# Layer 0's shift and scale computed transposed on TensorE, by column blocks, with the first projections accumulating over these blocks

## The chip, the cores and the metric

The kernel runs on one core of a Trainium2 chip. The metric is the device time of one execution in microseconds, the median of several runs. The kernel before takes 2007.55 us (three runs, 2006.95 to 2007.87).

## What is computed

The reference is one inference step of two trunk layers over 9 tiles of 128 tokens (tile 0 the context tokens, conditioned by `c_ctx`; tiles 1 to 8 the latent tokens, conditioned by `c`). D_MODEL is 1024. What this case touches is the head of each layer:

```python
mod = (silu(cvec) @ w_mod + b_mod)                 # w_mod: 1024 x 3072
shift, scale, gate = split(mod, 3)
h = rms_norm(x, g_pre) * (1.0 + scale) + shift
fx, fz, rq, rk, rv, rz, aq, ak, av, az, mg = split_columns(h @ w_in)
```

Three branches follow (Fourier mixing, retention, windowed attention), each gated, then a merge, an output projection and the residual.

## The kernel before

Activations are kept transposed, as `HH` and `HL` (model dimension on 128 partitions by 8 row blocks k, tokens along the free dimension): a rounded part and the remainder, so that a product with split weights `hi`, `lo` takes three matmuls (`proj_n`, L228 HH by hi, L229 HH by lo, L230 HL by hi). A weight unit is loaded into a `raw` buffer (two of them), split by ACT (L174, the rounded part) and POOL (L175, the remainder). Units of group 1 (columns `C_RK` to +512, two row blocks of 512 columns each) are loaded at L203 (`unit_n2`) in runs of 2 KB; units of the next sections at L188 (`unit_t`: 128 columns of all 1024 rows, runs of 512 bytes).

Layer 0 begins with `startup` (L285 on). SP issues all loads here, in the order of the program as its scheduler arranged it.

1. Three x tiles (L287) are loaded and normalised (`prep`: L254 sum of squares on ACT, L246 on DVE and L248 on POOL for the reciprocal root, L256 multiply on DVE), transposed on PE (L308), copied to `xT` by ACT (L309).
2. `w_mod` comes in 16 row blocks of 128 x 1024 (L325, `stage`, rows of 4 KB): eight of the scale, then eight of the shift. For the scale, DVE accumulates block by block for both conditionings (L335, L337), PE transposes (L345), DVE reduces (L346) and forms `sm` = (1 + scale) g_pre (L347, L348) and multiplies xT (L353). For the shift, PE multiplies `siluc` by the block (L360, output of 2 rows by 512 columns); the result is copied (L366), transposed (L369), and `sh` formed (L370). Then HH (ACT, L377) and HL (DVE, L378) of tiles 0 to 2.
3. Group 1 (`nat_group`, L519 on): for each of nine tiles, 24 matmuls of `proj_n` into one bank, then an evacuation with rotary embedding on DVE (`rope`, L491, L497, L501) and a store. Its first step loads the four weight units, in the midst of the shift's blocks (`GK`). Tiles 3 to 5 and 6 to 8 are loaded, prepared, and finished (`finish`: L387 on DVE, L388 HH on ACT, L390 HL on DVE or POOL) in chunks of three while earlier tiles are projected.

Behind group 1 come the DFT matmuls of the Fourier ring (L637) and then a long run of other projections (L218 to L220) and branches, in both layers, which the change leaves as it is.

Of the kernel before, what the change touches and what calls it, by code (L numbers as in the profile page):

```python
# [16 lines left out]
P = 128  # L17
D = 1024
# [13 lines left out]
GK = 3  # L32
# [50 lines left out]
def hybrid_step(ctx, tc, ins, cst, outs):  # L83
# [20 lines left out]
    def mk(pl, shape, tag, dt=F32, **kw):  # L104
        return pl.tile(shape, dt, tag=tag, name=nm(tag), **kw)
# [177 lines left out]
    def startup(first):  # L283
        with pool("st", side="right") as st:
            def load_x(t):  # L285
                xt = mk(st, [P, D], "x0", bufs=3)
                SP.dma_start(xt, ins["x_prompt"][0] if t == 0 else ins["x_sample"][0, (t - 1) * P : t * P, :])  # L287
                return xt

            xts = [load_x(t) for t in range(3)]  # L290
# [27 lines left out]
            wms = {}

            def stage(n):  # L320
                k, c0 = n % KT, 0 if n >= KT else D
                if n % 3 == 0:
                    wms["big"] = chunk("big", 2).rearrange("p a b -> p (a b)")
                wm = wms["big"][:, n % 3 * D : n % 3 * D + D]
                last_w[0] = SP.dma_start(wm, w_mod[0, k * P : (k + 1) * P, c0 : c0 + D]).ins  # L325
                return wm

            for k in range(KT):
                wm = stage(k)
                if k == 2:  # L330
                    SP.dma_start(bm, b_mod[0, 0 : 2 * D].rearrange("(s k p) -> p s k", p=P, k=KT))
                    SP.dma_start(gpr, g_pre[0].rearrange("(k p) -> p k", p=P))
                for s in range(2):
                    if k == 0:
                        DVE.tensor_scalar(dacc[s], wm, siluc[:, k, s : s + 1], None, op0=ALU.mult)  # L335
                    else:
                        DVE.scalar_tensor_tensor(  # L337
                            out=dacc[s], in0=wm, scalar=siluc[:, k, s : s + 1], in1=dacc[s], op0=ALU.mult, op1=ALU.add
                        )
            pr = mk(st, [P, KT, 2], "dred")  # L340
            for c in range(0, KT, 2):
                pt = (sc if c % 4 else sl)([P, 2, 2, P])
                for cc in range(2):
                    for s in range(2):
                        PE.transpose(pt[:, cc, s, :], dacc[s][:, (c + cc) * P : (c + cc + 1) * P], ident)  # L345
                DVE.tensor_reduce(pr[:, c : c + 2, :], pt, axis=AX.X, op=ALU.add)  # L346
            DVE.tensor_tensor(out=sm, in0=pr, in1=bm[:, 1, :].unsqueeze(2).to_broadcast([P, KT, 2]), op=ALU.add)  # L347
            DVE.scalar_tensor_tensor(  # L348
                out=sm, in0=sm, scalar=1.0, in1=gpr.unsqueeze(2).to_broadcast([P, KT, 2]), op0=ALU.add, op1=ALU.mult
            )  # L350
            for k in range(KT):
                for s, tok in ((0, slice(0, P)), (1, slice(P, CH))):
                    DVE.tensor_scalar(xT[:, k, tok], xT[:, k, tok], sm[:, k, s : s + 1], None, op0=ALU.mult)  # L353
            for k in range(KT):
                wm = stage(KT + k)
                if k == GK:
                    with tc.issue_after(last_w[0]):
                        next(first)
                for i in range(2):
                    PE.matmul(  # L360
                        macc[i], siluc[:, k, :], wm[:, i * 512 : i * 512 + 512], start=(k == 0), stop=(k == KT - 1)
                    )
            last = last_w[0]
            mr = mk(st, [P, D], "xh", bufs=2)
            for i in range(2):
                (DVE.tensor_copy if i else ACT.copy)(mr[:2, i * 512 : i * 512 + 512], macc[i])  # L366
                pt = tr([P, 4, 2])
                for c in range(4):
                    PE.transpose(pt[:, c, :], mr[:2, (4 * i + c) * P : (4 * i + c + 1) * P], ident[:2, :2])  # L369
                DVE.tensor_tensor(  # L370
                    out=sh[:, 4 * i : 4 * i + 4, :], in0=pt,
                    in1=bm[:, 0, 4 * i : 4 * i + 4].unsqueeze(2).to_broadcast([P, 4, 2]), op=ALU.add,
                )
            for s, tok in ((0, slice(0, P)), (1, slice(P, CH))):
                for k in range(KT):
                    b = sh[:, k, s : s + 1]
                    ACT.activation(HH[:, k, tok], xT[:, k, tok], AF.Identity, bias=b)  # L377
                    DVE.scalar_tensor_tensor(  # L378
                        out=HL[:, k, tok], in0=xT[:, k, tok], scalar=b, in1=f(HH[:, k, tok]),
                        op0=ALU.add, op1=ALU.subtract,  # L380
                    )
# [10 lines left out]
            xT = chunk("big", 2)  # L392
            for t in range(3, 6):
                with tc.issue_after(last):
                    xt = load_x(t)
                prep(t, xt, xT)
            next(first)
            finish(3, 6, 1, xT)
            xT = chunk("big", 2)
            for t in range(6, NT):  # L400
                with tc.issue_after(last):
                    xt = load_x(t)
                prep(t, xt, xT)
                next(first)
            finish(6, NT, 1, xT)
# [98 lines left out]
    for l in range(DEPTH):  # L504
# [56 lines left out]
        if l == 0:  # L561
            startup(g1)
# [730 lines left out]
```

## Time and profile before

| what | value |
|---|---|
| median of three runs | 2007.55 us |
| the profiled execution's own time | 2009.5 us |
| its span in the trace | 2007.7 us |
| mean granted TensorE clock | 0.989 of full speed |
| PE busy | 1955.6 us, 97% of the span |
| DVE, ACT, POOL busy | 51%, 34%, 27% of the span |
| chain that ended last | PE 87%, DMA 5%, DVE 4% |
| first projection of group 1 begins | 48.08 us |
| first matmul behind group 1 begins | 106.98 us |

The profiled execution lies 1.95 us above the median, and 1.8 us of it are outside the span. Times below are microseconds from the start of the span. A PE record of the form L228 lasts 0.39 us though the next begins 0.23 us later: matmuls are pipelined, and for work back to back the distance of the starts counts. The granted clock is given as a share of full speed: 1.00 is 2.4 GHz, 0.50 is 1.2 GHz.

### The profile page before, as it was taken

The numbers are of one execution on the slowest core, as the hardware profiler recorded it, in microseconds if no ns is written. First come the engines' busy times: TensorE is split into PE (matmuls) and PEld (weight loads), VectorE is DVE, ScalarE is ACT, GpSimd is POOL, SyncE is SP. The second block draws the span as 40 slices with busy tenths as digits, with TensorE's granted clock in tenths as the row PEclk, the third lists the DMA queues.
The fourth block names the chain that finished last, engine by engine and source line by source line (L and its number), as shares of the span: only waits on it lengthen the run. The fifth ranks groups of instructions, "written<-read, shape, count | busy, mean of one in ns | idle before, by whom it ended". The sixth has DMA issues, their size and how long they took to land.

```text
span 2007.7 us, 30798 instructions
## 1 busy us (share of the span) xinstructions
PE 1955.6 (97%) x11334; PEld 1815.4 (90%) x11334; DVE 1027.7 (51%) x2675; ACT 678.0 (34%) x1563; POOL 550.0 (27%) x424
## 2 busy tenths in 40 slices
PE   5999899999999999999999999999999999999998
PEld 2898788999999999999878978899999999999987
DVE  6726557556677774204675362444556655520411
ACT  3522111234454544214331211022445554421411
POOL 2222232112122222534441204122211222233342
PEclk8999999999999999999999999999999999999999
DMA  8323554353344333324344235234332433242142
GB/s 293 103 72 99 132 159 135 110 166 114 103 120 128 109 105 108 108 86 134 118 132 102 59 94 162 74 115 131 119 95 78 122 95 104 87 144 83 57 154 86
DMA packets 245191, 230.59 MB, mean 115 GB/s; under 512 B 37920, under 2 KB 215856, under 8 KB 244784
## 3 DMA queue, kind: packets, MB, share of 16 engines
q1 hardware_dynamic: 245040, 228.62, 37.9%
q8 instruction: 89, 1.46, 0.3%
q14 instruction: 62, 0.51, 0.1%
HBM read 170.14 MB, written 58.42 MB: 114 GB/s over the span
## 4 chain that ended last, share of the span: by engine, by line
PE 87%; DMA 5%; DVE 4%; issue 1%; ACT 1%; SPq 1%; POOL 0%; DVEq 0%; POOLq 0%; ACTq 0%
PE pj L218 13%; PE pj L220 13%; PE pj L219 13%; PE pj L228 5%; PE pj L229 5%; PE pj L230 5%; PE pv L1118 4%; PE tr L1111 3%; PE sl L1057 2%; PE sl L960 2%; PE sl L962 2%; PE sl L961 2%; PE pj L960 2%; PE pj L962 2%; PE pj L961 2%; PE sl L230 2%
## 5 line engine op out<-in xcount | busy, mean ns | idle before, releaser
L218 PE MATMUL pj<-HH,uh 128*128 128x384 f32 x1440 | 493.4, 343 | 8.9 <-DVE XL L653 3.9
L220 PE MATMUL pj<-HH,ul 128*128 128x384 f32 x1440 | 488.8, 339 | 0.0
L219 PE MATMUL pj<-HL,uh 128*128 128x384 f32 x1440 | 487.3, 338 | 0.0
L175 POOL TENSOR_TENSOR ul<-raw,uh 128x1024 fp32r<-128x1024 f32 x80 | 192.9, 2412 | 489.3 <-ACT uh L174 375.6
L218 PEld LDWEIGHTS pj<-HH,uh 128*128 128x128 f32 x1440 | 272.3, 189 | 13.2 <-DVE XL L653 4.2
L219 PEld LDWEIGHTS pj<-HL,uh 128*128 128x128 f32 x1440 | 272.1, 189 | 0.5
L220 PEld LDWEIGHTS pj<-HH,ul 128*128 128x128 f32 x1440 | 272.2, 189 | 0.3
L446 DVE SCALAR_TENSOR_TENSOR macc<-mw,siluc,macc 128x256 f32<-128x256 f32 x224 | 139.3, 664 | 10.5 <-DMA mw<-in_w_mod 10.5
L174 ACT CAST uh<-raw 128x1024 fp32r<-128x1024 f32 x80 | 84.0, 1050 | 168.0 <-PE pj L219 112.5
L228 PE MATMUL pj<-uh,HH 128*128 128x512 f32 x336 | 135.1, 403 | 5.2 <-DVE xh L1253 2.6
L229 PE MATMUL pj<-ul,HH 128*128 128x512 f32 x336 | 133.9, 399 | 0.0
L230 PE MATMUL pj<-uh,HL 128*128 128x512 f32 x336 | 133.7, 398 | 0.0
L1094 ACT ACTIVATE E<-E,NM 128x640 f32<-128x640 f32 (+1 forms) x128 | 101.8, 798 | 56.9 <-DVE NM L1090 56.4
L963 DVE SCALAR_TENSOR_TENSOR M<-M,sl 128x384 f32<-128x384 f32 x48 | 26.6, 554 | 183.1 <-PE sl L962 182.6
L1114 ACT CAST Eh<-tr 128x512 fp32r<-128x512 f32 (+1 forms) x136 | 76.2, 575 | 101.8 <-PE tr L1111 97.5
L1115 DVE TENSOR_TENSOR El<-tr,Eh 128x512 fp32r<-128x512 f32 (+1 forms) x136 | 90.3, 671 | 29.9 <-ACT Eh L1114 29.4
L975 POOL TENSOR_TENSOR mth<-mth,ml 128x384 f32<-128x384 f32 x48 | 52.0, 1084 | 180.0 <-DVE mth L963 100.0
L1075 DVE CUSTOM_DVE_ANT_0 E<-sl,mask,m 128x384 f32<-128x384 f32 (+1 forms) x128 | 71.6, 580 | 35.7 <-PE sl L1057 35.3
L1111 PE MATMUL tr<-ident,E 128*128 128x128 f32 x528 | 86.0, 272 | 0.0
L228 PEld LDWEIGHTS pj<-uh,HH 128*128 128x128 f32 x336 | 63.9, 190 | 20.0 <-DVE xh L1253 3.0
L963 DVE SCALAR_TENSOR_TENSOR mth<-mth,pj 128x384 f32<-128x384 f32 x96 | 52.9, 551 | 48.8 <-ACT mth L957 30.2
L230 PEld LDWEIGHTS pj<-uh,HL 128*128 128x128 f32 x336 | 63.8, 190 | 14.4 <-DVE HL L390 0.4
(316 smaller groups left out, 4125.3 us busy)
## 6 DMA issues: line engine op xcount, KB each, us to landing
raw<-in_w_in SPq DMA_DIRECT2D x84, 512.0 KB
scr_m<-mth SPq DMA_DIRECT2D x96, 192.0 KB
mw<-in_w_mod SPq DMA_DIRECT2D x128, 128.0 KB
scr_n<-ns SPq DMA_DIRECT2D x36, 256.0 KB
ml<-scr_m SPq DMA_DIRECT2D x48, 192.0 KB
mrow<-scr_m SPq DMA_DIRECT2D x16, 576.0 KB
big<-in_w_mod SPq DMA_DIRECT2D x16, 512.0 KB
raw<-in_w_out SPq DMA_DIRECT2D x16, 512.0 KB
```

Of the source, the lines that this page charges most:

```text
L174: ACT.copy(hi, raw)
L175: POOL.tensor_tensor(out=lo, in0=raw, in1=f(hi), op=ALU.subtract)
L218: PE.matmul(acc, hi[:, k, :], HH[:, k, tok], start=(k == 0), stop=False)
L219: PE.matmul(acc, hi[:, k, :], HL[:, k, tok], start=False, stop=False)
L220: i = PE.matmul(acc, lo[:, k, :], HH[:, k, tok], start=False, stop=(k == KT - 1))
L228: PE.matmul(acc, a, hi[:, k % 2, :], start=(k == 0), stop=False)
L229: PE.matmul(acc, a, lo[:, k % 2, :], start=False, stop=False)
L230: i = PE.matmul(acc, b, hi[:, k % 2, :], start=False, stop=(k == KT - 1))
L446: DVE.scalar_tensor_tensor(out=accs[s], in0=w, scalar=siluc[:, k, s : s + 1], in1=accs[s], op0=ALU.mult, op1=ALU.add,)
L1094: ACT.activation(Es[hh][:, 0:nk], srcs[hh], AF.Exp, bias=NM[t][:, hs + hh : hs + hh + 1], scale=0.125, accum_out=DEN[t][:, hs + hh : hs + ...
L1111: PE.transpose(pt[:, i, hh, :], Es[hh][:, (n + i) * P : (n + i + 1) * P], ident)
L1115: DVE.tensor_tensor(out=El[:, :w], in0=pt, in1=f(Eh[:, :w]), op=ALU.subtract)
```

## The change

In layer 0, `startup` is rewritten. Four x tiles come first (`ET`), with `cT`, `bm` and `gpr`. `w_mod` is then loaded by blocks of 128 columns with all 1024 rows: two loads for each block k (shift, scale; L299 of the changed kernel; 1024 runs of 512 bytes each) into five buffers, and a unit of `w_in` for group 1 for every two blocks. For each block, PE computes shift and scale transposed: 16 float32 matmuls with a 128 x 128 piece of `w_mod` as weights and the two columns of `siluc` as moving data (L346). DVE forms `sh` and `sm` of this block (L349, L350) and applies both to xT (L354, 128 and 384 columns); ACT rounds HH (L358, 128 x 512) and POOL takes HL (L359, 128 x 512). Then 12 matmuls (L364 to L366) add this block's share of the projections of tiles 0 to 3, in four banks. The matmuls of block k are ordered behind the projections of block k-2. Tiles 4 to 8 are loaded behind the last `w_mod` load, prepared (L320 sum of squares, L322 multiply in place, L327 transposes, L329 copies, one on ACT, one on DVE) and finished in pairs (L374, L375 on ACT, L377 on DVE or POOL), and projected as before; the ropes of group 1 are now L472, L478, L482. The accumulation over the scale on DVE, the transposes and reductions, and the 2 x 512 matmuls are gone.

```diff
-GK = 3
+ET = 4
...
-    def startup(first):
+    def startup(first, us, accs, unit):
...
-                xt = mk(st, [P, D], "x0", bufs=3)
+                xt = mk(st, [P, D], "x0", bufs=4)
...
+            def load_wm(k):
+                w = []
+                for j in range(2):
+                    wm = mk(st, [P, KT, P], "wm", bufs=5)
+                    c0 = j * D + k * P
+                    last_w[0] = SP.dma_start(wm, w_mod[0, :, c0 : c0 + P].rearrange("(k p) f -> p k f", p=P)).ins
+                    w.append(wm)
+                return w
+            xts = [load_x(t) for t in range(ET)]
...
+            wms = [load_wm(0)]
+            us.append(unit(0))
+            wms.append(load_wm(1))
...
-                xh = norm_x(st, xt)
+                ACT.activation(mk(st, [P, D], "x2"), xt, AF.Square, accum_out=ss)
+                r = rstd_of(st, ss, 1, 1.0 / D, EPS, "hr")
+                DVE.tensor_scalar(xt, xt, r, None, op0=ALU.mult)
...
-                    ACT.copy(xT[:, half * 4 : half * 4 + 4, t % 3 * P : (t % 3 + 1) * P], pt)
+                    out = xT[:, half * 4 : half * 4 + 4, n * P : (n + 1) * P]
+                    (DVE.tensor_copy if half else ACT.copy)(out, pt)
...
+            for t, b in enumerate((pj, pj, sl, sl)):
+                accs[t] = b([P, 512])
+            ends = []
             for k in range(KT):
+                if k + 2 < KT:
+                    if k % 2 == 0:
+                        us.append(unit(k // 2 + 1))
+                    wms.append(load_wm(k + 2))
+                pm = tr([P, 2, 2])
+                for j in range(2):
+                    for kk in range(KT):
+                        with tc.issue_after(ends[k - 2]) if k > 1 else nullcontext():
+                            PE.matmul(pm[:, j, :], wms[k][j][:, kk, :], siluc[:, kk, :], start=(kk == 0), stop=(kk == KT - 1))
+                DVE.tensor_scalar(sh[:, k, :], pm[:, 0, :], bm[:, 0, k : k + 1], None, op0=ALU.add)
+                DVE.tensor_scalar(sm[:, k, :], pm[:, 1, :], bm[:, 1, k : k + 1], gpr[:, k : k + 1], op0=ALU.add, op1=ALU.mult)
+                for s, tok in ((0, slice(0, P)), (1, slice(P, ET * P))):
+                    DVE.tensor_scalar(xT[:, k, tok], xT[:, k, tok], sm[:, k, s : s + 1], sh[:, k, s : s + 1], op0=ALU.mult, op1=ALU.add)
+                ACT.copy(HH[:, k, tok], xT[:, k, :])
+                POOL.tensor_tensor(out=HL[:, k, tok], in0=xT[:, k, :], in1=f(HH[:, k, tok]), op=ALU.subtract)
+                hi, lo = us[k // 2]
+                for t in range(ET):
+                    PE.matmul(accs[t], a, hi[:, k % 2, :], start=(k == 0), stop=False)
+                    PE.matmul(accs[t], a, lo[:, k % 2, :], start=False, stop=False)
+                    i = PE.matmul(accs[t], b, hi[:, k % 2, :], start=False, stop=(k == KT - 1))
+                ends.append(i.ins)
...
             next(first)
+            with tc.issue_after(last):
+                xts = [load_x(t) for t in range(ET, NT)]
+            for a, b in ((4, 6), (6, 8), (8, NT)):
+                xT = mk(st, [P, KT, 2 * P], "xT2")
+                for t in range(a, b):
+                    prep(t - a, xts[t - ET], xT)
+                finish(a, b, 1, xT)
...
             for t in range(NT):
+                if t in accs:
+                    acc = accs[t].rearrange("p (b c) -> p b c", b=8)
+                else:
+                    acc = pj([P, 8, 64])
+                    proj_n(us, t, acc.rearrange("p b c -> p (b c)"))
```

The four accumulators of tiles 0 to 3 are handed to `nat_group`, which skips `proj_n` for them; layer 1 is not changed.

**SP's queue of loads.** Before, in the stretch around the last `w_mod` blocks (`big` is a buffer of three row blocks, `raw` a weight unit, `x_` a token tile, `rope` a table, with the run counts at the end):

```order
L325 DMA big_244<-in_w_mod 128x1024 x3
L203 DMA raw_252<-in_w_in 128x2x512
L203 DMA raw_258<-in_w_in 128x2x512
L325 DMA big_279<-in_w_mod 128x1024 x3
L203 DMA raw_264<-in_w_in 128x2x512
L325 DMA big_289<-in_w_mod 128x1024
L287 DMA x_76_341<-in_x_sample 128x1024
L287 DMA x_83_363<-in_x_sample 128x1024
L287 DMA x_90_385<-in_x_sample 128x1024
L203 DMA raw_270<-in_w_in 128x2x512
L524 DMA rope_85<-cst_rope 128x8x128
```

Now, from the fourth unit of group 1 to the last `w_mod` block (`wm`):

```order
L203 DMA raw_376<-in_w_in 128x2x512
L299 DMA wm_298<-in_w_mod 128x8x128
L188 DMA raw_996<-in_w_in 128x8x128
L188 DMA raw_1002<-in_w_in 128x8x128
L188 DMA raw_1008<-in_w_in 128x8x128
L299 DMA wm_300<-in_w_mod 128x8x128
L299 DMA wm_337<-in_w_mod 128x8x128
L299 DMA wm_339<-in_w_mod 128x8x128
L299 DMA wm_382<-in_w_mod 128x8x128
L299 DMA wm_384<-in_w_mod 128x8x128
L299 DMA wm_421<-in_w_mod 128x8x128
```

and behind these:

```order
L299 DMA wm_423<-in_w_mod 128x8x128
L506 DMA rope_85<-cst_rope 128x8x128
L287 DMA x_92_531<-in_x_sample 128x1024
L287 DMA x_93_533<-in_x_sample 128x1024
L287 DMA x_94_535<-in_x_sample 128x1024
L287 DMA x_95_537<-in_x_sample 128x1024
```

Three units of the next section (L188) now stand ahead of the last seven `w_mod` loads, the second and third of them in buffers that the splits of two earlier units must first free; x tiles 4 to 7 stand behind the last `w_mod` load and the rope table.

**DVE.** Now, between blocks 5, 6 and 7 (`hrv` is the mean square of a tile; the last row is block 6's own):

```order
L246 TENSOR_SCALAR hrv_545<-ss_542 128x1
L322 TENSOR_SCALAR x_92_531<-x_92_531,hrr_547 128x1024
L246 TENSOR_SCALAR hrv_565<-ss_562 128x1
L322 TENSOR_SCALAR x_93_533<-x_93_533,hrr_567 128x1024
L246 TENSOR_SCALAR hrv_610<-ss_607 128x1
L322 TENSOR_SCALAR x_94_535<-x_94_535,hrr_612 128x1024
L246 TENSOR_SCALAR hrv_630<-ss_627 128x1
L322 TENSOR_SCALAR x_95_537<-x_95_537,hrr_632 128x1024
L349 TENSOR_SCALAR sh_71<-tr_460,bm_90 128x2
L350 TENSOR_SCALAR sm_72<-tr_460,bm_90,gpr_91 128x2
L354 TENSOR_SCALAR xT_123<-xT_123,sm_72,sh_71 128x128
L354 TENSOR_SCALAR xT_123<-xT_123,sm_72,sh_71 128x384
```

Four x tiles' normalisation (tiles 4 to 7) now stands between block 5's and block 6's shift and scale. On ACT their four sums of squares stand likewise ahead of the last two L358. A little further on, from the copy of the second half of tile 5 to the first HL of tiles 4 and 5 on DVE:

```order
L329 COPY xT_97_541<-tr_576 128x4x128
L246 TENSOR_SCALAR hrv_675<-ss_672 128x1
L472 TENSOR_TENSOR ns_728<-sl_206,rope_85 128x256
L478 TENSOR_TENSOR rpb_730<-sl_206,rope_85 128x8x16 x2
L374 TENSOR_SCALAR xT_97_541<-xT_97_541,sm_72,sh_71 128x256 x8
L322 TENSOR_SCALAR x_96_539<-x_96_539,hrr_677 128x1024
L482 TENSOR_TENSOR ns_728<-ns_728,rpb_730 128x256
L472 TENSOR_TENSOR ns_736<-sl_207,rope_85 128x256
L478 TENSOR_TENSOR rpb_738<-sl_207,rope_85 128x8x16 x2
L377 TENSOR_TENSOR HL_78<-xT_97_541,HH_77 128x256 x5
```

Between that copy and the first L377 now stand two tiles' ropes in part, the eight L374 and tile 8's normalisation.

**PE.** Now, from the last projection of block 5 to the first of block 6 (`tr` is the bank of a block's shift and scale):

```order
L366 MATMUL sl_207<-uh_294,HL_78 128x512
L346 MATMUL tr_460<-siluc_73,wm_382 128x2 x2
L346 MATMUL tr_460<-siluc_73,wm_384 128x2 x8
L346 MATMUL tr_495<-siluc_73,wm_421 128x2 x8
L346 MATMUL tr_495<-siluc_73,wm_423 128x2 x8
L364 MATMUL pj_204<-xh_378,HH_77 128x512
L365 MATMUL pj_204<-xl_379,HH_77 128x512
```

The matmuls of blocks 6 and 7 now both stand ahead of block 6's projections; behind those come the transposes of tile 4, then block 7's projections, the transposes of tiles 5 and 6, and tile 4's own projections.

## Rows read from the trace of the kernel before

**Rows 1.** The page: the span, and part 1, busy time with its share of the span and the instructions of each engine.

```profile
span 2007.7 us, 30798 instructions
PE 1955.6 (97%) x11334; PEld 1815.4 (90%) x11334; DVE 1027.7 (51%) x2675; ACT 678.0 (34%) x1563; POOL 550.0 (27%) x424
```

**Rows 2.** The view by windows, from the first matmul behind the first group of projections to the end. Columns: start:end and length, busy time of PE, PEld, DVE, ACT and POOL (instructions), granted TensorE clock as a share of full speed, share of the DMA engines, GB/s.

```profile
107.00:2007.70 1900.70, 1871.03 (x10984) 1757.67 (x10982) 954.52 (x2508) 632.04 (x1471) 521.82 (x398) 0.99 0.37 111
```

**Rows 3.** The timeline of PE: the first matmul of the first group of projections, the ring's DFT matmuls behind the last of the group, and the first matmul of the next section. Columns: start and length in us, engine, line, operation, output and inputs, tile, shape, number.

```profile
48.08 0.50 PE L228 MATMUL pj<-uh,HH 128*128 128x512 f32 x1 [0.16 <-ACT HH L377]
...
105.87 1.46 PE L637 MATMUL sl<-w,cdft 128*128 128x256 f32 x6
...
106.98 0.52 PE L218 MATMUL pj<-HH,uh 128*128 128x384 f32 x1
```

**Rows 4.** The timeline of PE in the middle of that group: the first and the last of a run of eight projection matmuls back to back, and the eight transposes behind them (same columns).

```profile
79.22 0.39 PE L228 MATMUL pj<-uh,HH 128*128 128x512 f32 x1
...
80.84 0.39 PE L229 MATMUL pj<-xl,HH 128*128 128x512 f32 x1
81.07 1.03 PE L308 MATMUL tr<-ident,xh 128*128 128x128 f32 x8
```

**Rows 5.** Windows (columns as in rows 2) in which the queue carries x tiles, and row blocks of `w_mod`, both in rows of 4 KB.

```profile
4.00:6.00 2.00, 0.00 (x0) 0.00 (x0) 0.00 (x0) 0.96 (x2) 0.00 (x0) 1.00 1.02 401
10.00:12.00 2.00, 1.57 (x8) 1.32 (x8) 1.02 (x2) 2.00 (x5) 0.00 (x0) 1.00 1.03 408
```

**Rows 6.** Windows (same columns) around the small loads of `cT`, and of `bm` and `gpr`.

```profile
7.00:9.00 2.00, 1.07 (x5) 1.08 (x6) 0.92 (x4) 0.66 (x3) 0.64 (x2) 1.00 1.02 73
12.50:15.00 2.50, 0.00 (x0) 0.00 (x0) 2.50 (x4) 0.03 (x1) 0.01 (x1) 0.92 1.03 62
```

**Rows 7.** One 512 KB load of runs of 512 bytes that goes alone: its issue on SP's queue, and the windows in which it moves (columns as in rows 3, then as in rows 2).

```profile
58.25 0.38 SPq L188 DMA_DIRECT2D raw<-in_w_in  x1
...
59.00:59.50 0.50, 0.50 (x6) 0.50 (x5) 0.50 (x1) 0.00 (x0) 0.50 (x1) 1.00 0.15 46
59.50:60.50 1.00, 1.00 (x8) 0.86 (x8) 1.00 (x1) 0.59 (x1) 1.00 (x1) 1.00 0.86 239
60.50:61.50 1.00, 1.00 (x6) 0.77 (x5) 1.00 (x1) 0.97 (x2) 0.58 (x1) 1.00 0.86 260
61.50:62.00 0.50, 0.50 (x4) 0.41 (x3) 0.13 (x1) 0.50 (x2) 0.00 (x0) 1.00 0.06 23
```

**Rows 8.** The timeline: the issue of the first x tile, and the first instruction that waits for it.

```profile
1.18 0.42 SPq L287 DMA_DIRECT2D x<-in_x_prompt  x1
...
5.04 1.06 ACT L254 ACTIVATE xh<-x 128x1024 f32<-128x1024 f32 x1 [3.02 <-DMA x<-in_x_prompt]
```

**Rows 9.** Groups by line and by shape in the first 107 us. Columns: line, engine, operation, output<-inputs, shapes, number | busy us, mean ns of one | idle us just before them, and what ended it.

```profile
L254 ACT ACTIVATE xh<-x 128x1024 f32<-128x1024 f32 x9 | 9.6, 1061 | 3.1 <-DMA x<-in_x_prompt 3.0
L246 DVE TENSOR_SCALAR hrv<-ss 128x1 f32<-128x1 f32 x9 | 1.3, 146 | 8.9 <-ACT xh L254 8.8
L248 POOL TENSOR_TENSOR hrr<-hrv,mhalf 128x1 f32<-128x1 f32 x9 | 6.2, 687 | 25.2 <-DVE hrv L246 25.2
L256 DVE TENSOR_SCALAR xh<-x,hrr 128x1024 f32<-128x1024 f32 x9 | 8.9, 984 | 2.5 <-POOL hrr L248 2.5
L353 DVE TENSOR_SCALAR xT<-xT,sm 128x128 f32<-128x128 f32 x8 | 2.2, 276 | 0.0
L387 DVE TENSOR_SCALAR big<-big,sm,sh 128x384 f32<-128x384 f32 x16 | 9.2, 650 | 5.3 <-ACT big L309 5.3
L309 ACT COPY big<-tr 128x512 f32<-128x512 f32 x12 | 6.6, 586 | 8.5 <-PE tr L308 8.5
L174 ACT CAST uh<-raw 128x1024 fp32r<-128x1024 f32 x4 | 4.2, 1046 | 17.0 <-DMA raw<-in_w_in 17.0
L175 POOL TENSOR_TENSOR xl<-raw,xh 128x1024 fp32r<-128x1024 f32 x3 | 7.2, 2386 | 3.4 <-ACT xh L174 3.4
L491 DVE TENSOR_TENSOR ns<-pj,rope 128x256 f32<-128x256 f32 x8 | 3.3, 417 | 3.5 <-PE pj L230 3.5
L497 DVE TENSOR_TENSOR rpb<-pj,rope 128x128 f32<-128x128 f32 x16 | 3.8, 278 | 0.0
L353 DVE TENSOR_SCALAR xT<-xT,sm 128x256 f32<-128x256 f32 x8 | 4.8, 606 | 0.0
L501 DVE TENSOR_TENSOR ns<-ns,rpb 128x256 f32<-128x256 f32 x8 | 5.0, 623 | 0.1
L378 DVE SCALAR_TENSOR_TENSOR HL<-xT,sh,HH 128x256 fp32r<-128x256 f32 x8 | 3.3, 480 | 0.0
```

**Rows 10.** Matmuls of plain float32: one group of the whole run by line and shape (columns as in rows 9), and eight records of it on the timeline (as in rows 3).

```profile
L868 PE MATMUL tr<-kvq,A 128*128 128x64 f32 x144 | 18.4, 269 | 0.0
...
313.40 1.00 PE L868 MATMUL tr<-kvq,A 128*128 128x64 f32 x8
```

**Rows 11.** Windows (columns as in rows 2) in which the granted clock fell or rose.

```profile
14.50:18.00 3.50, 0.00 (x0) 0.00 (x0) 3.50 (x6) 0.00 (x0) 1.46 (x1) 0.51 0.95 298
45.50:48.50 3.00, 0.83 (x6) 0.66 (x7) 2.64 (x12) 1.22 (x5) 0.55 (x1) 1.00 1.09 361
48.50:52.00 3.50, 3.50 (x15) 3.01 (x14) 3.24 (x10) 3.50 (x10) 0.13 (x1) 0.53 1.10 296
52.00:55.00 3.00, 3.00 (x14) 2.47 (x13) 3.00 (x9) 3.00 (x9) 0.42 (x1) 0.98 0.32 67
```

More of the change, by code (lines that the diff above doesn't have):

```diff
@@ L318, in startup @@
[L318 to L326, printed above, removed]
-            for k in range(KT):
[L329 to L361, printed above, removed]
-                    )
@@ L363, in startup @@
-            last = last_w[0]
[L364 to L381, printed above, removed]
+                        PE.transpose(pt[:, kk, :], xt[:, k * P : (k + 1) * P], ident)
@@ new lines, in prep @@
+                    out = xT[:, half * 4 : half * 4 + 4, n * P : (n + 1) * P]
+                    (DVE.tensor_copy if half else ACT.copy)(out, pt)
+            xT = mk(st, [P, KT, ET * P], "xT")
+            for t in range(ET):
+                prep(t, xts[t], xT)
+            for t, b in enumerate((pj, pj, sl, sl)):
+                accs[t] = b([P, 512])
+            ends = []
+            for k in range(KT):
+                if k + 2 < KT:
[6 more added lines that the diff above has]
+                        with tc.issue_after(ends[k - 2]) if k > 1 else nullcontext():
+                            PE.matmul(
+                                pm[:, j, :], wms[k][j][:, kk, :], siluc[:, kk, :], start=(kk == 0), stop=(kk == KT - 1)
+                            )
+                DVE.tensor_scalar(sh[:, k, :], pm[:, 0, :], bm[:, 0, k : k + 1], None, op0=ALU.add)
+                DVE.tensor_scalar(
+                    sm[:, k, :], pm[:, 1, :], bm[:, 1, k : k + 1], gpr[:, k : k + 1], op0=ALU.add, op1=ALU.mult
+                )
+                for s, tok in ((0, slice(0, P)), (1, slice(P, ET * P))):
+                    DVE.tensor_scalar(
+                        xT[:, k, tok], xT[:, k, tok], sm[:, k, s : s + 1], sh[:, k, s : s + 1], op0=ALU.mult, op1=ALU.add
+                    )
+                tok = slice(0, ET * P)
+                ACT.copy(HH[:, k, tok], xT[:, k, :])
+                POOL.tensor_tensor(out=HL[:, k, tok], in0=xT[:, k, :], in1=f(HH[:, k, tok]), op=ALU.subtract)
+                hi, lo = us[k // 2]
+                for t in range(ET):
+                    tk = slice(t * P, (t + 1) * P)
+                    a, b = HH[:, k, tok][:, tk], HL[:, k, tok][:, tk]
+                    PE.matmul(accs[t], a, hi[:, k % 2, :], start=(k == 0), stop=False)
+                    PE.matmul(accs[t], a, lo[:, k % 2, :], start=False, stop=False)
+                    i = PE.matmul(accs[t], b, hi[:, k % 2, :], start=False, stop=(k == KT - 1))
+                ends.append(i.ins)
@@ L390, in finish @@
                     eng.tensor_tensor(out=HL[:, k, tok], in0=hf, in1=f(HH[:, k, tok]), op=ALU.subtract)
[L392 to L396, printed above, removed]
-            next(first)
[L398 to L405, printed above, removed]
+            next(first)
+            with tc.issue_after(last):
[5 more added lines that the diff above has]
+                finish(a, b, 1, xT)
         for _ in first:
@@ L517, in hybrid_step, with nat_group @@
             SP.dma_start(ropet, cst["rope"].rearrange("(t p) f -> p t f", p=P))
-        def nat_group(cols, r_heads, c0):
-            us = [unit_n2(w_in, k2, cols) for k2 in range(4)]
+        def nat_group(cols, r_heads, c0, us=None, accs={}):
+            if us is None:
+                us = [unit_n2(w_in, k2, cols) for k2 in range(4)]
             if l == 0 and c0 == 0:
@@ L558, in nat_group @@
                 yield
-        g1 = nat_group([(C_RK, 512)], 4, 0)
         if l == 0:
-            startup(g1)
+            us1, accs1 = [], {}
+            g1 = nat_group([(C_RK, 512)], 4, 0, us1, accs1)
+            startup(g1, us1, accs1, lambda k2: unit_n2(w_in, k2, [(C_RK, 512)]))
+        else:
+            g1 = nat_group([(C_RK, 512)], 4, 0)
         for _ in g1:
```

22 lines of the change are left out of this document (8 added, 14 removed).

## The prediction

> **What bounds the kernel now.** I read the page first: PE is busy 97% of the span [rows 1]. The windows then say where the other 3% lie: behind group 1, from 107.0 us on, PE works 1871.0 of 1900.7 us [rows 2]. So from there on nothing but PE sets the time, and whatever the head of layer 0 gains or loses goes through to the end nearly whole. The timeline of PE gives the marks of the head [rows 3]: group 1 begins at 48.08 and the next section at 106.98. The order of instructions behind that point stays, so the whole effect is the shift of that second mark. Group 1 itself is full: 216 projections at the distance of the starts, (80.84 - 79.22) / 7 = 0.231 us [rows 4], are 49.9, 48 transposes at 1.03 / 8 = 0.129 are 6.2, the DFT matmuls 2.0; that is 58.1 of the 58.9 us, the rest being a stretch at half clock [rows 11]. Ahead of 48 the kernel waits for loads. The change lets projections of four tiles begin there; the question is when the last tiles' data arrive and who stands behind them.
>
> **Prices of a load.** 512 KB in rows of 4 KB move at 401 to 408 GB/s [rows 5], 1.3 us; I take the same for the 2 KB runs of `w_in`. In runs of 512 bytes a lone load took 0.15 x 0.5 + 0.86 + 0.86 + 0.06 x 0.5 = 1.8 us of all engines [rows 7]. The bounds are 1.3 (as 4 KB rows) and 2.5 (from 59.0 to 61.5); I take 1.8, since those are the same engines' busy time for the same shape. The first two small loads cost the queue 2.0 x (1 - 73/405) = 1.6 us, the other two 2.5 x (1 - 62/405) = 2.1 [rows 6]. From issue to the first byte takes about 1.0 (58.25 to past 59.0) [rows 7]; the first x tile, issued at 1.18, was used at 5.04 [rows 8], which leaves 3.86 - 1.0 - 1.3 - 0.2 (the identity ahead of it) = 1.3 from the last byte to use; I take 1.2.
>
> **By the Trainium skill, DMA: Bandwidth & Descriptors, Specifications, transfers of 512 bytes and more reach line rate.** The row of this trace disagrees, 512 KB in 1.8 us being 290 GB/s [rows 7]; by that rule the sum would be that of the second rival below.
>
> **The queue, added up.** First byte 2.1, identity 0.2, four x tiles 5.2, small loads 3.8: 11.3. Then nine `w_mod` loads (16.2) and four units (5.2): 32.7. Now the order puts three units of the next section ahead of the last seven `w_mod` loads. The first lands at 34.5 and is usable at 35.7; its buffer comes free behind ACT's split, 1.05, and POOL's, 2.39 [rows 9], at 39.1. Only then can SP issue the third: first byte 40.1, done 41.9 (the second lies in between). The seven `w_mod` loads, 12.6, end at 54.5; the rope table, also runs of 512 bytes, 56.3; x tiles 4 to 7, 61.5, usable 62.7.
>
> **DVE and ACT behind that.** Normalising tiles 4 to 7 stands ahead of block 6's shift and scale on DVE, so block 6 waits for tile 7: sum of squares 1.06, 0.15, 0.69, 0.98 [rows 9], with 0.6 for handing over: 66.2. Block 6: two small operations at 0.15, then 0.28 and 0.65 on xT [rows 9], HH 0.59 (price of a 128 x 512 copy): first projection of block 6 at 68.1.
>
> **PE up to there.** A two-column float32 matmul with 128 x 128 weights isn't in the trace. The nearest is L868, 64 columns: 144 records for 72 matmuls of the program, and eight records take 1.00 us, the last of them 0.269, so they start (1.00 - 0.27) / 7 = 0.104 apart [rows 10], which makes 0.21 for a matmul; bounds 0.10 (one record) and 0.27 (the mean length of one). At 0.21 a block's 16 are 3.4; its 12 projections at 0.231 are 2.8. The first block is usable at 11.3 + 3.6 + 1.2 = 16.1. PE gets to the scale of block 4 at 16.1 + 4 x 3.4 + 1.7 + 3 x 2.8 = 39.8, but that load (first of the seven) is usable at 44.9: a wait of 5.1. From there 1.7 + 3 x 3.4 + 3 x 2.8 = 20.3 to the end of block 7's matmuls: 65.2. DVE's 68.1 is later and decides.
>
> **To the end of group 1.** Two blocks of projections 5.5, tile 4's transposes 1.0, waits for HL 0.3: 74.9; tile 5's transposes 75.9. Then DVE, in its order: the copy 0.59, 0.15, a rope's 0.42 and 2 x 0.28, eight L374 of 256 columns at 0.61, tile 8's 0.98, 0.62, 0.42, 2 x 0.28, the first HL 0.48 [rows 9]: 9.6, so the first HL of tile 4 is there at 85.5. PE meanwhile does tile 6's transposes and four projections, 1.9, and waits 7.7. What is left: 116 projections, 26.8, two tiles' transposes 2.1, DFT 2.0: 116.4. After such waits the clock falls: PE had 0.83 us of work in the 3 us to 48.5, and 48.5 to 52.0 then ran at 0.53 [rows 11], which costs 1.7; I charge it once: **118.1**. Against 106.98 that is **+11.1**. DVE's accumulation (16 passes) and the 2 x 512 matmuls that go away lay beside loads: worth nothing by themselves. Evacuating four tiles at the block's end instead of one by one costs nothing more than the ropes counted above. The profiled execution would go from 2009.5 to 2020.6; it lies 1.95 above the median of the runs, so the forecast is 2007.55 + 11.1 = **2018.7**.
>
> **Rivals.**
> 1. *Forecast.* Its own range: each 0.1 us on the price of a 512-byte load moves 20 loads, 2 us; 1.6 to 2.1 gives -4 to +6, and DVE's row of 9.6 may be 2 shorter or longer: 2013 to 2027.
> 2. *Runs of 512 bytes go at the rate of 4 KB rows when many stand in the queue.* For it: the trace shows such a load alone only, and its ends weigh [rows 7]. Against: 0.86 is its steady share, at 239 and 260 GB/s [rows 7]. Then 28.2 after the ninth, 34.1 for the split, 36.4, 45.5, 52.0 for tile 7, DVE ready at 58.6; PE, from 15.1 with no wait, ends block 7's matmuls at 15.1 + 27.2 + 16.8 = 59.1, so block 6 begins 9.0 earlier than forecast: +2.1, 2009.7, no change that can be told. This is the side of not slower, and it decides from a last `w_mod` landing before about 47 instead of 54.5. If PE's wait of 7.7 for tile 4 shrinks too (DVE's prices include a busy POOL beside it) [rows 9] it goes below: by 6 or more, faster.
> 3. *PE at 1.2 GHz in the block stage.* For it: between 14.5 and 18.0, with PE idle, the clock fell to 0.51, and it was 0.53 after the idle of 48.5 [rows 11]; the new stage is short bursts with waits for data and for DVE. Against: PE has work for 44 of the 49 us between 16.1 and 65.2. With half of this work at half clock the matmuls end at 16.1 + 44 x 1.5 = 82.1, 14.0 later than 68.1: +25.1, 2032.7. All of it: 104, +47, 2054.6.
> 4. *The shift is soaked up.* Behind 107 us PE is idle 29.7 us in all [rows 2]; if a good part of it were waits for things that don't move, the time would stay, 2007.5. Against: the loads there are issued as buffers come free, so they shift as well.
>
> **By the Trainium skill, TensorE: Matmul & The Clock Gate, HAM oscillation — how this bites in real kernels, a kernel whose bursts are shorter than the wait for the next slice runs each burst at the low clock.** That would be rival 3 in its full form; the rows agree for the idle start, and none shows it for short bursts.
>
> **Chances.** Forecast 0.57, rival 2 0.18, rival 3 0.19, rival 4 0.06. A measurement of this kernel can tell 0.2%, 4.0 us. Of rival 2 I give 0.06 to faster (below 2003.5), 0.09 to no change, 0.03 to the slow side; rival 4 is no change. Slower: 0.57 + 0.19 + 0.03 = 0.79; same 0.15; faster 0.06. The range runs from rival 2's time less a little, 2009, to rival 3's half form, 2034; it leaves out rival 2's lower part, rival 4 and the full rival 3, about 0.2.
>
> **What would show it.** In the profile after: the first two-column matmul near 16 us and 0.21 apart; three L188 issues on SP between 33 and 40, ahead of seven `w_mod` loads, the last landing near 54.5; PE waiting from about 65 to 68 for block 6's HH while DVE waits for x tiles; then some 8 us of PE's waits for tile 4's HL; the first L218 near 118. The forecast is wrong if the w_mod loads take 1.3 each (rival 2), if the clock stands at 0.5 between 18 and 65 (rival 3), or if block 6's projections begin before tile 7 is normalised.

## The result and the profile after

The changed kernel takes 2031.31 us (median of four, 2028.86 to 2036.55) against 2007.25 for the kernel before beside it: a ratio of 1.0116, 95% interval 1.0103 to 1.0128, or 24 us slower. Slower was forecast, by 11.1 us; the size is more than twice that. The time is near that of the third rival in its half form (2032.7).

The page of the changed kernel begins so (its profiled run took 2036.55 us, the longest of the four):

```profile
span 2034.4 us, 31188 instructions
...
PE 1987.3 (98%) x11534; PEld 1858.5 (91%) x11534; DVE 1012.5 (50%) x2673; ACT 673.5 (33%) x1553; POOL 558.8 (27%) x435
```

against [rows 1]: PE works 32 us more. The window behind group 1 (columns as in [rows 2]) says where not:

```profile
133.00:2034.40 1901.40, 1870.58 (x10984) 1757.00 (x10983) 956.48 (x2515) 632.90 (x1472) 521.26 (x398) 0.99 0.37 111
```

That is 1901.4 us against 1900.7 [rows 2]. So nearly the whole difference lies ahead of the mark, as the prediction had it. PE's timeline up to there (columns as in [rows 3]; L327 are transposes of the first four tiles, L346 the two-column matmuls, two records each, L364 a projection of HH by hi; only the first projections of each block are shown):

```profile
12.54 4.92 PE L327 MATMUL tr<-ident,x 128*128 128x128 f32 x20 [1.87 <-DVE xT L329]
17.25 13.65 PE L346 MATMUL tr<-siluc,wm 128*128 128x2 f32 x64
30.76 0.77 PE L364 MATMUL pj<-uh,HH 128*128 128x512 f32 x1
31.34 0.63 PE L365 MATMUL pj<-ul,HH 128*128 128x512 f32 x1
31.76 0.63 PE L364 MATMUL pj<-uh,HH 128*128 128x512 f32 x1
...
35.97 1.40 PE L346 MATMUL tr<-siluc,wm 128*128 128x2 f32 x12
37.22 0.48 PE L364 MATMUL pj<-uh,HH 128*128 128x512 f32 x1
37.54 0.39 PE L365 MATMUL pj<-ul,HH 128*128 128x512 f32 x1
37.77 0.39 PE L364 MATMUL pj<-uh,HH 128*128 128x512 f32 x1
...
40.04 8.64 PE L346 MATMUL tr<-siluc,wm 128*128 128x2 f32 x52
48.54 0.77 PE L364 MATMUL pj<-xh,HH 128*128 128x512 f32 x1
...
53.42 1.39 PE L346 MATMUL tr<-siluc,wm 128*128 128x2 f32 x12
54.68 0.48 PE L364 MATMUL pj<-xh,HH 128*128 128x512 f32 x1
...
57.56 9.06 PE L346 MATMUL tr<-siluc,wm 128*128 128x2 f32 x52
66.48 0.77 PE L364 MATMUL pj<-uh,HH 128*128 128x512 f32 x1
...
70.97 1.40 PE L346 MATMUL tr<-siluc,wm 128*128 128x2 f32 x12
72.22 0.48 PE L364 MATMUL pj<-uh,HH 128*128 128x512 f32 x1
...
75.07 6.36 PE L346 MATMUL tr<-siluc,wm 128*128 128x2 f32 x52
81.29 0.77 PE L364 MATMUL pj<-xh,HH 128*128 128x512 f32 x1
...
96.13 0.50 PE L228 MATMUL pj<-uh,HH 128*128 128x512 f32 x1 [1.98 <-ACT HH L375]
...
100.25 0.80 PE L230 MATMUL pj<-uh,HL 128*128 128x512 f32 x1 [2.93 <-DVE HL L377]
...
133.06 0.52 PE L218 MATMUL pj<-HH,uh 128*128 128x384 f32 x1
```

The mark, the first L218, is at 133.06 where it was 106.98 [rows 3]. From 17.25 to 90 PE has no gap that the timeline shows. Read the distances of the starts: the first 64 two-column records take 13.65 us, (13.65 - 0.42) / 63 = 0.21 us apart; the twelve at 35.97 are (1.40 - 0.28) / 11 = 0.10 apart. The projections at 31.34 and 31.76 start 0.43 apart, those at 37.54 and 37.77 0.23, the distance of [rows 4]. So PE goes at half speed all through the first long run of two-column matmuls and for most of the projections right behind it, and at full speed after that. It was at half speed before that run began: 20 transposes take 4.92 us behind a wait of 1.87, where eight took 1.03 in [rows 4]. The other three long runs (40.04, 57.56 and 75.07) begin at full speed and fall to half on the way, and most of the projections right behind them go at half too. The granted clock, in the windows (columns as in [rows 2]), says the same from 42 us on:

```profile
17.50:28.00 10.50, 10.50 (x51) 10.50 (x51) 3.85 (x5) 2.71 (x3) 4.77 (x2) 1.00 1.17 317
30.70:35.90 5.20, 5.20 (x13) 4.14 (x14) 1.52 (x4) 1.66 (x2) 3.80 (x3) 1.00 0.94 290
42.00:53.00 11.00, 11.00 (x46) 10.03 (x47) 2.29 (x8) 1.24 (x2) 2.54 (x2) 0.53 0.88 235
...
60.00:70.00 10.00, 10.00 (x39) 9.26 (x40) 2.17 (x8) 1.24 (x2) 2.55 (x2) 0.50 0.91 268
75.00:80.00 5.00, 5.00 (x47) 4.96 (x46) 2.62 (x7) 1.01 (x3) 1.40 (x3) 1.00 0.02 5
80.50:86.50 6.00, 6.00 (x17) 4.79 (x17) 1.14 (x4) 0.62 (x1) 1.67 (x2) 0.50 0.00 0
```

It is 0.53 and 0.50 (1.2 GHz) over most of the second and third long runs and the projections behind them, 1.00 for the first 5 us of the fourth, and 0.50 from 80.5 on, with PE busy all of each window. (Busy means that the records follow one another without a gap; it does not say how much of the array works.) Ahead of 36 the column says 1.00 though the starts lie as far apart as at half clock. The first clock record of this trace stands only at 35.9, where the distances change, so ahead of it the distances are what I read.

SP's queue (columns as in [rows 3]) with its waits for PE from 41 to 64 us (us in total, times, longest), and DVE's wait for tile 7:

```profile
32.06 8.89 SPq L188 DMA_DIRECT2D raw<-in_w_in  x3
41.00 22.61 SPq L299 DMA_DIRECT2D wm<-in_w_mod  x7
...
64.28 2.59 SPq L287 DMA_DIRECT2D x<-in_x_sample  x4
...
SPq L299 <- PE tr L346: 19.3, 6, 8.9
```

```profile
77.06 0.75 DVE L322 TENSOR_SCALAR x<-x,hrr 128x1024 f32<-128x1024 f32 x1 [0.73 <-POOL hrr L248]
77.73 0.21 DVE L349 TENSOR_SCALAR sh<-tr,bm 128x2 f32<-128x2 f32 x1
```

The three L188 stand where the order put them, from 32 to 41. But the seven `w_mod` loads behind them take 22.6 us to issue, 19.3 of them in six waits for one of the five buffers, which PE's matmuls free. Tile 7 is normalised at 77.8 and block 6's shift follows at once; PE is through with block 7's matmuls only at 81.3.

### The profile page after: what moved, and what is told of

It reads as the page before. It is cut to its first block, busy times and chain, and to the rows that moved or that the text cites. A ratio compares the mean times of both kernels' runs of the same rounds, so it can differ in the third digit from the quotient of the medians.

```text
span 2034.4 us, 31188 instructions
## 1 busy us (share of the span) xinstructions
PE 1987.3 (98%) x11534; PEld 1858.5 (91%) x11534; DVE 1012.5 (50%) x2673; ACT 673.5 (33%) x1553; POOL 558.8 (27%) x435
## 4 chain that ended last, share of the span: by engine, by line
PE 84%; DVE 4%; DMA 4%; issue 1%; ACT 1%; SPq 1%; POOL 1%; DVEq 0%; POOLq 0%; ACTq 0%
PE pj L218 13%; PE pj L220 13%; PE pj L219 13%; PE pj L228 5%; PE pj L229 5%; PE pj L230 5%; PE pv L1106 4%; PE tr L1099 3%; PE sl L1045 2%; PE sl L948 2%; PE sl L950 2%; PE sl L949 2%; PE sl L229 2%; PE sl L228 2%; PE pj L948 2%; PE sl L230 2%
## 5 line engine op out<-in xcount | busy, mean ns | idle before, releaser
L218 PE MATMUL pj<-HH,uh 128*128 128x384 f32 x1440 | 493.8, 343 | 7.8 <-DVE grz L237 3.1
L218 PEld LDWEIGHTS pj<-HH,uh 128*128 128x128 f32 x1440 | 272.4, 189 | 12.2 <-ACT mth L945 4.2
L228 PE MATMUL pj<-uh,HH 128*128 128x512 f32 x320 | 127.9, 401 | 6.5 <-ACT kv L531 2.3
L230 PE MATMUL pj<-uh,HL 128*128 128x512 f32 x320 | 127.4, 398 | 2.9 <-DVE HL L377 2.9
L229 PE MATMUL pj<-ul,HH 128*128 128x512 f32 x320 | 127.2, 398 | 0.0
```

The costliest lines, as they stand in the source:

```text
L218: PE.matmul(acc, hi[:, k, :], HH[:, k, tok], start=(k == 0), stop=False)
L228: PE.matmul(acc, a, hi[:, k % 2, :], start=(k == 0), stop=False)
L229: PE.matmul(acc, a, lo[:, k % 2, :], start=False, stop=False)
L230: i = PE.matmul(acc, b, hi[:, k % 2, :], start=False, stop=(k == KT - 1))
```

## The experiments

Three theories. **C**, the clock: runs of two-column matmuls leave TensorE at 1.2 GHz, themselves and the projections behind them. **W**: each record costs what loading 128 x 128 float32 weights costs, whatever else. **Q**: the loads behind the next section's units set the pace, as the prediction's sum had it. All twelve kernels start from the changed one (their line numbers shift by a few). The mark is the first L218-like matmul in each profile; ratios are to the kernel before, run beside it, whose time differed between calls (2000.6 to 2007.6).

| kernel | ratio, 95% interval | block 7's matmuls end | mark |
|---|---|---|---|
| before | 1 | - | 106.98 |
| changed | 1.0116 (1.0103 to 1.0128) | 81.4 | 133.06 |
| e1_ord64 | 1.0037 (1.0024 to 1.0049) | 69.4 | 113.71 |
| e2_fine2 | 1.0207 (1.0184 to 1.0229) | 101.4 | 152.43 |
| e3_lean | 0.9969 (0.9956 to 0.9982) | 52.3 | 100.20 |
| e4_fxlate | 1.0128 (1.0110 to 1.0146) | 79.6 | 130.60 |
| e5_ord2 | 1.0117 (1.0099 to 1.0136) | 78.5 | 129.09 |
| e6_ord16 | 1.0101 (1.0081 to 1.0121) | 78.3 | 129.17 |
| e7_alt64fx | 1.0035 (1.0023 to 1.0047) | 65.4 | 115.49 |
| e8_fine64fx | 1.0057 (1.0038 to 1.0077) | 75.0 | 122.97 |
| e9_alt64 | 1.0016 (1.0007 to 1.0025) | 64.6 | 110.91 |
| e10_r64fx | 0.9994 (0.9985 to 1.0003) | 58.1 | 104.71 |
| e11_r64fxo | 1.0005 (0.9995 to 1.0014) | 61.9 | 110.67 |
| e12_r64 | 0.9993 (0.9982 to 1.0004) | 58.8 | 106.62 |

**e1_ord64 and its control e5_ord2.** Both hold PE's order to that of the changed kernel; they differ in the moving operand.

```diff
-    PE.matmul(pm[:, j, :], wms[k][j][:, kk, :], siluc[:, kk, :], ...)    # e5: 2 columns
+    PE.matmul(pm[:, j, :], wms[k][j][:, kk, :], silw[:, kk], ...)        # e1: siluc repeated to 64 columns
```

> Edit: the moving operand of the shift and scale matmuls is siluc repeated to 64 columns (output 128x64, two columns used); PE's order is held to that of the changed kernel. Theory C (the clock: runs of two-column matmuls leave TensorE at 1.2 GHz, themselves and the projections behind them): 256 records stay about 0.104 us apart, the granted clock stays near 1.00 from 17 to 66 us, block 7's matmuls end near 65 to 67 instead of 81.3, the next section begins near 118 to 120 instead of 133.1, the time is 2017 to 2021 us. Theory W (each record costs what loading 128x128 float32 weights costs, whatever moves) and theory Q (the w_mod loads behind three units of the next section set the pace): no change, 2027 to 2036 us.

> Control for the first experiment: the same way of holding PE's order, but two columns as in the changed kernel. Theory C (the clock): as the changed kernel, 2027 to 2036 us, with the records 0.21 us apart in stretches. If the way the order is held had made the first experiment faster and not the columns: 2010 to 2020 us.

PE's timeline of e1, runs of 52 records:

```profile
35.00 5.91 PE L355 MATMUL tr<-silw,wm 128*128 128x64 f32 x52
...
50.79 5.91 PE L355 MATMUL tr<-silw,wm 128*128 128x64 f32 x52
...
63.47 5.91 PE L355 MATMUL tr<-silw,wm 128*128 128x64 f32 x52
```

the same runs in e5 (the fence below), and two windows of e1 (columns as in [rows 2]):

```profile
36.56 6.23 PE L353 MATMUL tr<-siluc,wm 128*128 128x2 f32 x52
...
52.43 8.25 PE L353 MATMUL tr<-siluc,wm 128*128 128x2 f32 x52
...
69.90 8.62 PE L353 MATMUL tr<-siluc,wm 128*128 128x2 f32 x52
```

```profile
53.00:60.00 7.00, 7.00 (x53) 6.49 (x51) 2.29 (x8) 1.24 (x2) 2.55 (x2) 1.00 0.93 255
60.00:70.00 10.00, 9.38 (x72) 8.73 (x70) 2.74 (x8) 4.60 (x8) 1.65 (x3) 1.00 0.63 231
```

With 64 columns each run of 52 takes 5.91 us, 0.11 a record; with two, 6.23, 8.25 and 8.62 for the same weights. The first run, of 64 records, begins at half speed in both, behind the same transposes; it takes 7.50 us in e1, 10.75 in e5 and 13.65 in the changed kernel. Work that is 32 times as wide takes less time, so W falls as the cause of the loss (at full clock a record does cost nearly the same with 2 columns and with 64). The windows of e1 show 1.00 where the changed kernel had 0.50. The mark moves from 129.09 to 113.71, the ratio from 1.0117 to 1.0037: two thirds of the loss. The control shows that holding the order is not what did it. Block 7's matmuls end 2 to 4 us later than C had it, with waits of 0.64 to 1.54 us for HH and HL ahead of them, and the mark is 4 to 6 us earlier. One thing moved beside the columns: with 64 the scheduler put the three L188 one by one between the `w_mod` loads. e4 bears on that, and so does e7: both have these units behind x tile 7, and with 64 columns (and a stricter order) the mark is at 115.49, with two at 130.60.

**e6_ord16.** As e1, with `silw` of 16 columns.

> Edit: as the first experiment, with 16 columns instead of 64. Theory C with the columns as what counts in proportion: 16 are nearer to 2 than to 64, the clock falls in the runs of these matmuls and the time is 2024 to 2036 us. Theory C with anything wider than a pair of columns enough: as with 64 columns, 2008 to 2020 us. Theory W (weight loads alone) is already against the first experiment.

1.0101, mark 129.17: as with two columns, so the first reading of C.

**e2_fine2.** Two columns, PE's order finely mixed.

```diff
+    for k in range(2, KT):
+        for g in range(4):
+            mods(k, 4 * g, 4 * g + 4)          # four two-column matmuls
+            proj(k - 2, 3 * g, 3 * g + 3)      # three projections
```

> Edit: still two columns, but PE's order alternates finely: four two-column matmuls, then three projections of the block two before, through the stage, instead of runs of 16 to 32 matmuls. Theory C: what stands between matters; if the projections hold the clock the stage ends near 66 and the time is 2014 to 2021 us, if the mixture is at 1.2 GHz all through, the stage ends near 95 to 105 and the time is 2045 us or more. Theories W and Q: no change beyond 4 us, 2027 to 2036 us.

PE's timeline, and a window of the same stretch (columns as in [rows 2]):

```profile
12.59 4.92 PE L327 MATMUL tr<-ident,x 128*128 128x128 f32 x20 [1.42 <-DVE xT L329]
...
42.05 0.63 PE L380 MATMUL sl<-ul,HH 128*128 128x512 f32 x1
42.48 0.63 PE L380 MATMUL sl<-uh,HL 128*128 128x512 f32 x1
42.90 1.70 PE L353 MATMUL tr<-siluc,wm 128*128 128x2 f32 x8
```

```profile
42.00:53.00 11.00, 11.00 (x43) 9.89 (x41) 0.79 (x3) 0.62 (x1) 1.27 (x1) 1.00 0.51 143
```

The projections start 0.43 apart here and to the end of the stage at 101.4; eight two-column records take 1.70 us with the last one's 0.4, so (1.70 - 0.42) / 7 = 0.18 apart. That is C's second branch, with the mark 19 us behind that of the changed kernel. The stage begins at half speed here too, as the 20 transposes show, and PE comes back to full speed only at 103.9, when projections run alone. So the trace shows no fall: mixed in, the two-column matmuls keep every projection at half speed, where in the changed kernel PE came back each time in a stretch of projections alone. The granted-clock column says 1.00 in this stretch, which the distances refute; the first clock record of this trace stands at 104.1.

**e3_lean.** Two two-column matmuls for a block instead of sixteen: it leaves out seven eighths of each sum and only prices the work.

```diff
-    for kk in range(KT):
+    for kk in range(1):
```

> Leaves out 7 of the 8 row blocks in every shift and scale product (2 two-column matmuls for a block instead of 16); all loads stay. Theories C and W: PE is no longer late, DVE's wait for x tile 7 sets block 6 (first projection near 66 to 69), the next section begins near 116 to 119 and the time is 2015 to 2020 us. Theory Q: the loads set the pace, so no change beyond 4 us, 2027 to 2036 us.

The mark is at 100.20, 6.8 ahead of the kernel before, and the time 2001.19 against 2007.58. All theories had it too slow: I had DVE's wait for tile 7 as the floor, near 68; here block 7's few matmuls are through at 52.3. So the loads can come earlier than the prediction's queue sum had them, and with an eighth of the shift and scale products on PE, accumulating over blocks would pay.

**e4_fxlate.** The three units behind x tile 7.

```diff
+    with tc.issue_after(x_last[0]) if l == 0 else nullcontext():
         us = [unit_t(w_in, c0) for c0 in (C_FX, C_FX + P, C_FZ, C_FZ + P)]
```

> Edit: the three units of the next section are issued behind x tile 7 instead of ahead of the last seven w_mod loads. Theories C and W: PE works without a gap in the stage, so nothing changes beyond 4 us, 2027 to 2036 us. Theory Q: the w_mod loads and the x tiles come some 9 us earlier, and so does the end: 2020 to 2025 us.

1.0128, mark 130.60: no change to the end. Q falls for the changed kernel: PE, not the queue, was late.

**e7_alt64fx, e8_fine64fx, e9_alt64.** With the clock mostly held, does the queue count? e7 alternates 16 and 12 and has e4's edit; e9 is e7 without it; e8 is e7 in e2's order. In e9 the scheduler put the three units one by one between the `w_mod` loads, at 32.8, 39.4 and 43.1, so three in a row with the clock held was not run.

> Edit: 64 columns, PE's order strictly 16 of these matmuls and 12 projections in turn, and the three units of the next section issued behind x tile 7. With the clock held, the prediction's second term (units ahead of w_mod loads, then x tiles, then DVE) should count: block 7's matmuls end near 61 to 64 (69.4 with 64 columns alone), the next section begins near 102 to 108, 2003 to 2010 us. If the queue is not what is late even then: 2012 to 2018 us, as with 64 columns alone.

> Edit: as the seventh experiment (64 columns, 16 and 12 in turn) but with the three units of the next section where the scheduler put them, between w_mod loads. If the prediction's queue term counts once the clock is held: the last w_mod load and x tile 7 come 5 to 9 us later than in the seventh, and the next section begins 4 to 8 us later, near 120 to 123. If not: within 2 us of 115.5.

> Edit: as the one before, with the fine order (four of these matmuls, three projections). It covers PE's waits for HH and HL of a block with the next block's matmuls: the next section begins near 100 to 106, 2001 to 2008 us. If the waits in the stage come from loads and not from HH and HL, as the one before or 2 us slower.

The timeline of SP, POOL and DVE in e7, with SP's waits for PE from 32 to 52 us, then the timeline of SP and DVE in e9:

```profile
31.91 19.43 SPq L302 DMA_DIRECT2D wm<-in_w_mod  x7
...
52.01 2.71 SPq L288 DMA_DIRECT2D x<-in_x_sample  x4
...
SPq L302 <- PE tr L358: 17.6, 7, 4.1
...
66.40 2.40 POOL L176 TENSOR_TENSOR ul<-raw,uh 128x1024 fp32r<-128x1024 f32 x1
...
66.47 2.88 DVE L327 TENSOR_SCALAR x<-x,hrr 128x1024 f32<-128x1024 f32 x1 [0.73 <-POOL hrr L249]
```

```profile
51.25 17.43 SPq L287 DMA_DIRECT2D x<-in_x_sample  x5
...
65.86 0.75 DVE L324 TENSOR_SCALAR x<-x,hrr 128x1024 f32<-128x1024 f32 x1 [0.73 <-POOL hrr L248]
```

e9's mark is 4.6 us ahead of e7's, the other way from what I expected (in the times the two intervals just overlap). In both the x tiles are issued at 51 to 52: the seven loads of e7 still take 19.4 us, paced by PE through the five buffers, so moving the units brought no load forward. What it moved was POOL's split of a unit, now at 66.40, beside DVE's multiply of tile 7, which took 2.88 us and ended 0.55 behind it; in e9 the same multiply takes 0.75. With that, tile 4's first HL lets PE go on at 81.91 in e7 and at 78.72 in e9, 3.2 us apart; the other 1.4 lie behind it, where PE goes at half speed until 88.0 in e7 and until 81.9 in e9. That the split makes the multiply slow is read from these rows, not tested by itself. e8 ran at half clock for 20 us in spite of its 64 columns (PE's timeline, then windows with columns as in [rows 2]):

```profile
29.16 0.53 PE L385 MATMUL pj<-uh,HL 128*128 128x512 f32 x1 [1.26 <-POOL HL L374]
...
28.00:36.00 8.00, 6.84 (x27) 6.22 (x27) 1.32 (x1) 1.63 (x3) 4.69 (x3) 0.59 1.10 292
36.00:42.00 6.00, 6.00 (x24) 5.42 (x24) 2.56 (x4) 1.60 (x2) 3.64 (x2) 0.50 0.33 95
```

The fall comes right behind two waits, 0.56 us for DVE and this one of 1.26 for POOL, as the falls of [rows 11] come behind waits; it is not the kind that the long runs show. Then the clock stays low with PE busy without a gap, until 49.9, and stands at 1.00 from 53 to 60 in the same fine order. So a wide operand does not always keep the clock through waits; why it came back so late stays open.

**e10_r64fx, e11_r64fxo, e12_r64.** If PE's own work is what is left, halve it: ACT rounds each block of `w_mod` and the 64-column matmuls take one record.

```diff
+    wr = mk(st, [P, KT, P], "wr", F32R, bufs=2)
+    ACT.copy(wr, wm)
```

> Edit: as the seventh experiment, but ACT rounds each block of w_mod to the matmul's rounded type (fp32r) and the 64-column matmuls take one record each instead of two; shift and scale lose the low bits of w_mod and siluc; w_mod has three buffers and two rounded ones. Theory C with PE's own work as the bound: some 13 us less of PE work, block 7's matmuls end near 52 to 58 if the loads keep up, the next section begins near 103 to 108 (100.2 with seven eighths of the products left out), about -2 to -8 us against the seventh. If the loads with three buffers, or ACT's 16 more casts, set the pace: block 7's matmuls end near 60 to 66 and there is no change beyond 3 us.

> Edit: as the one before, with the scheduler's own order on PE. Expected within 3 us of it; faster by 2 to 5 us if the strict order holds projections back.

> Edit: as the tenth experiment (64 columns, one record each from rounded w_mod, 16 and 12 in turn), but with the three units of the next section left between the w_mod loads, since in the ninth that was faster than behind the x tiles: there POOL's splits of these units had made DVE's multiply of x tile 7 wait (2.88 us for 0.75). Expected: next section near 100 to 104 (104.7 in the tenth), 1 to 4 us below the kernel before. If ACT's casts or three buffers then set the pace: 104 to 107, no difference from before.

Block 7's matmuls end at 58 to 62, and the times are those of the kernel before: the ratios lie within 0.07% of 1, the intervals within 0.2%. (In e10 and e12 the DFT matmuls, 1.5 us, come behind the mark.) None is faster than before by what can be measured, and e12 did not gain from e9's lesson.

## Why the prediction was wrong

The step that failed is "At 0.21 a block's 16 are 3.4; its 12 projections at 0.231 are 2.8", and the 65.2 that it led to: both are prices at full clock. Term by term to the end of block 7's matmuls:

| term | forecast | changed kernel |
|---|---|---|
| first two-column matmul | 16.1 | 17.25 |
| 128 two-column matmuls | 27.2 | 40.9 |
| projections of blocks 0 to 5 | 16.8 | 5.2 + 2.8 + 4.9 + 2.9 + 4.5 + 2.9 = 23.2 |
| wait for block 4's scale | 5.1 | none |
| end | 65.2 | 81.3 |

(The projections' times are from a block's first start to the start of the matmuls behind it; 40.9 is what is left of 81.3 - 17.25.) At full clock the price per matmul was right: 0.10 to 0.11 for a record, as estimated from [rows 10]; with the clock held e9 ends this stage at 64.6. The first stretch, from 17.25 to 35.97, took 18.7 us for what the forecast priced at 9.6; it began at half speed behind waits, and e1 shows that it need not have stayed there. The rest of the excess lies in runs that fell while PE was busy.

Behind it the forecast had block 6 held by DVE until 68.1; it was held by PE until 81.3: 13.2 more. From there to the mark, forecast 50.0, measured 51.8, with waits of 1.98 and 2.93 for tile 4 and two shorter ones, 6.2 in all where 7.7 were forecast, and a stretch at half clock. 13.2 + 1.8 = 15.0, the difference of 133.06 and 118.1.

The queue's step was right in its order and wrong in what paces it: the three units stood at 32 to 41, near the forecast's 33 to 40, yet the loads behind them waited for buffers, not for the queue; e4 shows that the units cost nothing there, and e9 that one by one they cost nothing with the clock held either. Rival 2 did not come: from 17.5 to 28 the queue moved 317 GB/s, 1.65 us for 512 KB, nearer to 1.8 than to 1.3. Nor did rival 4, since behind the mark the time is the same. DVE's hold of block 6 happened (block 6's shift follows tile 7's multiply at once) but did not decide.

Rival 3 was the right one, at 0.19 where it should have had most: its half form put block 7's end at 82.1 and the time at 2032.7; measured 81.3 and 2031.3. The half was worked out from no row, so the close fit is luck, and its reason, short bursts with waits, covers at most the first stretch. What I set against it was that PE has work for 44 of 49 us. That was the mistake: PE was busy without a gap and still ran at 1.2 GHz. The Trainium skill, TensorE: Matmul & The Clock Gate, HAM oscillation — how this bites in real kernels, tells of bursts that wait for DMA; no such wait stands in the stage here, so its rule, read to the letter, would have let this kernel off. The trace goes further than the page. In the kernel before, every fall that I had read came with PE idle or nearly so [rows 11], and I took idleness for the only cause. What makes a run fall after 2 to 3 us or after 5, as here, or lets e5's first run rise for a while, these runs do not show.

## What to carry to other kernels

Do not price long runs of matmuls with very few moving columns at full clock, nor the projections that follow them: here they cost 1.5 and 1.4 times as much, and a busy PE is no sign of a full clock. Where such products are needed, try a wider moving operand (64 columns took 0.11 us a record here, two took 0.10 at full clock; 16 did not help), and compare the distances of the starts, not the busy share. A load that stands late in a queue is only late if the queue, and not a buffer that somebody must free, holds it.

## What the hardware showed that I had not expected

- 1.2 GHz with PE busy for 10.00 of 10 us (60 to 70 us of the changed kernel, granted clock 0.50).
- The granted-clock column read 1.00 in stretches where starts were 0.43 us apart instead of 0.23 (30.7 to 35.9 in the changed kernel, 42 to 53 in e2); in both traces the first clock record comes only behind them (35.9 and 104.1).
- At half clock from the start, two-column matmuls four at a time between three projections kept PE there for more than 60 us without a gap (e2).
- 64 moving columns in float32 took 0.11 us a record, two took 0.10 at full clock and 0.21 at half.
- A DVE multiply of 128 x 1024 took 0.75 us alone (e9) and 2.88 beside a split on POOL, ending 0.55 behind it (e7).
